# The DeltaNet's triangular inverses in 32x32 blocks, two per partition on DVE alone, joined to 128 by small TensorE products

## The chip, the cores and the metric

The kernel runs on one NeuronCore of a Trainium2 chip, as one launch. The metric is the time of that launch on the device in microseconds (us); three runs before gave a median of 2909.26 us (2909.12 to 2916.06). The engines are named as in the profile: PE is TensorE (matrix products), DVE is VectorE, ACT is ScalarE, POOL is GpSimd, SP is SyncE, whose queue issues most of the DMAs.

## The reference

A trunk of two layers for 256 tokens of width 2048, all in float32: the first layer mixes with MLA attention, the second with a gated DeltaNet; each is followed by a SwiGLU FFN and a gated embedding. The change lies in the DeltaNet, in the chunked delta rule, of which this is the core (32 value heads, 4 chunks of 64 tokens, head width 128):

```python
def chunk_gated_delta_rule(q, k, v, g, beta):
    ...                                        # C = 64 tokens a chunk
    decay = jnp.where(tril, jnp.exp(jnp.where(tril, diff, 0.0)), 0.0)
    L = jnp.where(strict, jnp.einsum('bhncd,bhnsd->bhncs', k_beta, k) * decay, 0.0)
    A = L + jnp.eye(C, dtype=f32)
    rhs = jnp.concatenate([v_beta, k_beta * jnp.exp(g)[..., None]], axis=-1)
    sol = lax.linalg.triangular_solve(A, rhs, left_side=True, lower=True, unit_diagonal=True)
    ...
    def step(state, inp):
        q_c, k_c, u_c, w_c, g_c, a_c = inp
        v_new = u_c - jnp.einsum('bhcd,bhde->bhce', w_c, state)
        o = (jnp.einsum('bhcd,bhde->bhce', q_c * jnp.exp(g_c)[..., None], state)
             + jnp.einsum('bhcs,bhse->bhce', a_c, v_new))
        ...
```

The kernel works with chunks of 128 tokens, two of them for the 256 tokens, which is the same mathematics. For each of 32 heads and 2 chunks it needs the inverse of I + L, where L is strictly lower triangular and 128x128: 64 such inverses.

## The kernel before

**The weights' products.** `linear` streams every weight matrix through the core. A tile `raw` of 4 x 128 rows by 512 columns (1 MB, three buffers) is loaded by SP. ACT rounds it to its high part `wh` (line 231), DVE subtracts to get the low part `wl` (line 232, "the split"), each in pieces of two k-tiles with five buffers. PE then makes twelve products a piece, three for each of two k-tiles and two token tiles (lines 240 to 242). After each piece `tick()` lets the generators in the lists `fill` and `back` put one more step of side work into the program. A scheduler then lays down one fixed order for each engine, and every engine runs its own in order. An evacuation takes the sums out of PSUM at the end of a block of 512 columns.

**The DeltaNet.** After the projections of q and k, `group` makes L^T for eight groups of four heads (tile `LT`) and stores the diagonal 64x64 blocks in DRAM as `Ld`, one block to a row of 128 (64 inverses, two blocks each), and the off-diagonal 64x64 blocks as `Md`. The next stretch of PE's work is the z projection in eight blocks (gg 0 to 7, the last one 256 columns wide, evacuated by `gate_z`) and the first block of the v projection, `first_v`. Beside it `lanes` computes the inverses of the 128 diagonal blocks by forward substitution, one 64x64 block to a partition: at each of 63 steps one product `pr` (line 790) and one difference `X` (line 792) over the rows below. The columns are divided: the first 12 (`KSPLIT`) go to DVE, the other 52 to POOL. ACT then copies the result out, transposed (`XT`) and straight (`XC`), and stores it as `XTd` and `Xd`.

**The joins and the scans.** For each group of eight inverses `tbuild` loads the two diagonal blocks of the inverse into `tt`, and with `d64` and `m64` makes the off-diagonal block by two stages of eight fp32 products in PE (line 824), with a copy by ACT (line 828) and one by DVE (line 831) behind them. A join for group gg + 2 is put into `back` when the scan of group gg nears its end. `scan` applies the delta rule to one group; the rest of the v projection and the output projection `w_out` run beside the scans.

Of the kernel before, what the change touches and what calls it, by code (L numbers as in the profile page):

```python
# [42 lines left out]
KSPLIT = 12  # L43
# [5 lines left out]
LAGX = 4  # L49
LSLOW = (8, 56)  # L50
# [16 lines left out]
def trunk(ctx: ExitStack, tc: tile.TileContext, a: dict, out, plan=("mla", "ffn", "ple", "gdn", "ffn", "ple"), first=0):  # L67
# [25 lines left out]
    # constants  # L93
# [10 lines left out]
    # residual stream  # L104
# [8 lines left out]
    # norm gains as columns  # L113
# [12 lines left out]
    def make_xT(src, gains):  # L126
        """src(t): [128 tokens, 512]; gives the two exact parts of its transpose times the gains, [128, 4, 256] each."""
# [36 lines left out]
    class Norm:  # L164
        """Parts of (h * gain)^T and, per token, 1/rms(h)."""
# [53 lines left out]
    def linear(xs, W, kt, blocks, evac, row0=0, need=None):  # L219
        """ps[t] = x[t] @ W[row0:, c0:c0+n] in float32, from exact 12-bit parts of both operands."""  # L220
# [38 lines left out]
    # ------------------------------------------------------------------ MLA  # L259
    def mla(j, nrm, nxt, mc):  # L260
# [6 lines left out]
        # rotary tables  # L267
# [26 lines left out]
        # upper bounds on scores: +BIG where a key may be seen, -BIG where not  # L294
# [6 lines left out]
        # latents  # L301
# [32 lines left out]
        # the keys' rotary part  # L334
# [138 lines left out]
    # ------------------------------------------------------------------ FFN  # L473
# [78 lines left out]
    # ------------------------------------------------------------------ GDN  # L552
    def gdn(j, nrm, nxt, mc, ctx):
# [20 lines left out]
        # tri[s, c] = 1 where s <= c  # L574
# [67 lines left out]
        def project(c0):  # L642
            """[tokens, 512] of the projection, before the convolution."""
# [32 lines left out]
        def l2(acc, dst):  # L676
            """dst = 1 / sqrt(sum of squares + eps) of the block's 4 heads; gives what is under the root."""
# [33 lines left out]
        def group(gg, rho, kap, E):  # L711
            """L^T and intra^T of value heads 4gg..4gg+3; rho, kap: [dk, 4 heads, 256 tokens]."""
# [59 lines left out]
        def lanes(pool):  # L772
            """Inverses of the 64x64 diagonal blocks of I + L, one per partition, by forward substitution."""
            L3 = pool.tile([P, 64, 64], F32, name="LL")
            nc.sync.dma_start(out=L3, in_=Ld)
            cols = []
            for eng, lo, hi in ((nc.vector, 0, KSPLIT), (nc.gpsimd, KSPLIT, 64)):
                X3 = pool.tile([P, 64, hi - lo], F32, name=f"X{lo}")
                nc.gpsimd.memset(X3, 0.0)
                nc.gpsimd.memset(X3.rearrange("p i k -> p (i k)")[:, lo * (hi - lo):hi * (hi - lo):hi - lo + 1], 1.0)  # L780
                cols.append((eng, lo, hi, X3, p4("pr")))
            for _ in range(8):
                yield
            for jj in range(63):
                ni = 63 - jj
                for eng, lo, hi, X3, pr in cols:
                    nk = min(jj + 1, hi) - lo
                    if nk > 0:
                        p3 = pr[:, 0:ni * nk].rearrange("p (i k) -> p i k", k=nk)
                        eng.tensor_mul(out=p3, in0=L3[:, jj, jj + 1:64].unsqueeze(2).to_broadcast([P, ni, nk]),  # L790
                                       in1=X3[:, jj, 0:nk].unsqueeze(1).to_broadcast([P, ni, nk]))
                        eng.tensor_sub(out=X3[:, jj + 1:64, 0:nk], in0=X3[:, jj + 1:64, 0:nk], in1=p3)  # L792
# [5 lines left out]
            for c in range(4):
                XT, XC = (p4(n).rearrange("p (a b) -> p a b", b=64) for n in ("XT", "XC"))
                b0 = 16 * c  # L800
                for _, lo, hi, X3, _ in cols:
                    s, e = max(lo, b0), min(hi, b0 + 16)
                    if s < e:
                        nc.scalar.copy(out=XT[:, s - b0:e - b0, :], in_=X3[:, :, s - lo:e - lo].rearrange("p i k -> p k i"))
                    nc.scalar.copy(out=XC[:, :, lo:hi], in_=X3[:, b0:b0 + 16, :])
                nc.scalar.dma_start(out=XTd[:, b0:b0 + 16, :], in_=XT)
                nc.scalar.dma_start(out=Xd[:, b0:b0 + 16, :], in_=XC[0:64])
                yield

        def tbuild(gg):  # L810
            """(I + L)^-T of a group's 8 chunks (head, chunk), from the inverses of the diagonal blocks."""
            tt = tts[gg % 2]
            for half in range(2):
                s, lane = slice(64 * half, 64 * half + 64), 64 * half + 8 * gg
                nc.sync.dma_start(out=tt[s, :, s], in_=XTd[lane:lane + 8].rearrange("m k i -> k m i"))
            nc.sync.dma_start(out=d64, in_=Xd[8 * gg:8 * gg + 8].rearrange("m i k -> i m k"))
            nc.sync.dma_start(out=m64[:, :, 64:128], in_=Md[gg])
# [13 lines left out]
            nc.vector.tensor_copy(out=tt[0:64, :, 64:128], in_=prods(64, w2[64:128], tt[64:128, :, 64:128], 64)[0:64])  # L831
# [48 lines left out]
        m64 = build.tile([64, 8, P], F32, name="m64")  # L880
# [182 lines left out]
```

## Time and profile before

| | before |
|---|---|
| median of three runs | 2909.26 us (2909.12 to 2916.06) |
| profiled execution: span from first to last instruction | 2911.4 us (the page gives no other time of it) |
| PE busy | 2829.5 us (97%), 13233 product records |
| DVE busy | 1733.8 us (60%) |
| ACT busy | 1368.2 us (47%) |
| POOL busy | 320.9 us (11%) |
| moved by DMA | 538.99 MB, 185 GB/s in the mean |

A product of `linear` is one record for PE; an fp32 product of the DeltaNet appears as two records. Records overlap, so a record's length is not its price; the price is the distance of two starts. Idle time of an engine that is not the bottleneck costs nothing.

### The profile page before, as it was taken

The page shows a single profiled execution, that of the slowest core. Times are in us where ns is not written, and L with a number is a line of the kernel's source. Part 1 is how long each engine was busy: PE and PEld are TensorE (multiplying, and loading weights), DVE is VectorE, ACT ScalarE, POOL GpSimd, SP SyncE. Part 2 cuts the span into 40 slices and gives each one's busy share as a digit, 9 for nine tenths or more (in the row PEclk, how much of TensorE's full clock was granted, in tenths as well). Part 3 has the DMA queues.
Part 4 walks back from the last instruction along what each step waited for, and adds up shares of the span by engine and source line. Part 5 has one row for each costly group of instructions (what it writes and reads, how often), then busy time and mean ns, then how long its engine had stood idle before and what let it go on. Part 6 is the DMA issues. An engine that isn't in the chain of part 4 may idle for free.

```text
span 2911.4 us, 33700 instructions
## 1 busy us (share of the span) xinstructions
PE 2829.5 (97%) x13233; PEld 2344.8 (81%) x13233; DVE 1733.8 (60%) x2112; ACT 1368.2 (47%) x1824; POOL 320.9 (11%) x358
## 2 busy tenths in 40 slices
PE   8999999999999999999957999999999999999999
PEld 8778888888888888778745788888888888888887
DVE  5665554544554666576799566767555554555654
ACT  6765444344344556555312544444544344434453
POOL 1330000000000000323696000000000000000000
PEclk9999999999999999999978999999999999999999
DMA  6335555555555555676623865554555555555554
GB/s 218 126 116 177 188 188 188 196 194 188 188 192 183 204 188 187 196 230 196 221 98 123 269 190 174 195 183 168 188 188 188 189 193 194 190 188 190 200 188 145
DMA packets 300241, 538.99 MB, mean 185 GB/s; under 512 B 39561, under 2 KB 60722, under 8 KB 299954
## 3 DMA queue, kind: packets, MB, share of 16 engines
q1 hardware_dynamic: 299186, 533.69, 55.6%
q10 hardware_dynamic: 896, 3.15, 0.3%
q8 instruction: 104, 1.70, 0.2%
q14 instruction: 55, 0.45, 0.0%
HBM read 516.84 MB, written 19.96 MB: 184 GB/s over the span
## 4 chain that ended last, share of the span: by engine, by line
PE 85%; DVE 7%; DMA 3%; ACT 2%; issue 1%; POOL 1%; SPq 0%; ACTq 0%; DVEq 0%; POOLq 0%
PE mm L240 26%; PE mm L242 26%; PE mm L241 26%; DVE wl L232 3%; DVE pr L790 2%; PE tr L135 2%; DVE X L792 1%; DMA raw<-in_gdn_w_in 1%; PE tr L917 1%; PE tr L824 1%; PE tr L923 1%; ACT wh L231 1%; PE tr L722 0%; PE S L412 0%; PE tr L660 0%
## 5 line engine op out<-in xcount | busy, mean ns | idle before, releaser
L232 DVE TENSOR_TENSOR wl<-raw,wh 128x1024 fp32r<-128x1024 f32 (+2 forms) x952 | 1176.3, 1240 | 982.1 <-ACT wh L231 976.4
L231 ACT CAST wh<-raw 128x1024 fp32r<-128x1024 f32 (+2 forms) x952 | 982.9, 1036 | 1306.4 <-PE mm L242 1178.2
L241 PE MATMUL mm<-wl,xh 128*128 128x512 f32 (+2 forms) x3776 | 1470.9, 390 | 51.8 <-DVE wl L232 51.5
L240 PE MATMUL mm<-wh,xh 128*128 128x512 f32 (+2 forms) x3776 | 1483.9, 393 | 5.2 <-ACT wh L231 5.1
L242 PE MATMUL mm<-wh,xl 128*128 128x512 f32 (+2 forms) x3776 | 1466.9, 389 | 0.0
L241 PEld LDWEIGHTS mm<-wl,xh 128*128 128x128 f32 x3776 | 715.6, 190 | 200.2 <-DVE wl L232 66.0
L240 PEld LDWEIGHTS mm<-wh,xh 128*128 128x128 f32 x3776 | 715.5, 190 | 149.0 <-ACT wh L231 6.2
L242 PEld LDWEIGHTS mm<-wh,xl 128*128 128x128 f32 x3776 | 715.4, 189 | 140.4 <-DVE xl L447 0.2
L102 POOL TENSOR_TENSOR re<-re,neghalf 128x2 f32<-128x2 f32 x2 | 1.4, 696 | 1350.2 <-DVE re L524 1350.2
L790 POOL TENSOR_TENSOR pr<-LL,X 128x51 f32<-128x51 f32 (+25 forms) x51 | 75.5, 1481 | 17.7 <-DMA LL<-Ld 13.8
L792 POOL TENSOR_TENSOR X<-X,pr 128x51 f32<-128x51 f32 (+25 forms) x51 | 73.4, 1439 | 4.0
L790 DVE TENSOR_TENSOR pr<-LL,X 128x240 f32<-128x240 f32 (+59 forms) x63 | 58.1, 923 | 4.0 <-DMA LL<-Ld 2.5
L792 DVE TENSOR_TENSOR X<-X,pr 128x240 f32<-128x240 f32 (+59 forms) x63 | 57.5, 913 | 1.5
L254 DVE TENSOR_TENSOR h<-h,mm 128x512 f32<-128x512 f32 x88 | 56.7, 680 | 2.3 <-PE mm L242 2.3
L144 ACT ACTIVATE xh<-tr,ncol 128x256 fp32r<-128x256 f32 x104 | 46.9, 475 | 19.6 <-PE tr L135 12.5
L145 DVE SCALAR_TENSOR_TENSOR xl<-tr,ncol,xh 128x256 fp32r<-128x256 f32 x104 | 47.4, 482 | 4.6 <-ACT xh L144 2.8
L102 POOL TENSOR_TENSOR rs<-rs,neghalf 128x2 f32<-128x2 f32 x6 | 4.8, 806 | 384.1 <-DVE rs L177 384.1
L970 POOL TENSOR_TENSOR r8o<-r8o,rq 128x8 f32<-128x8 f32 x8 | 5.2, 656 | 358.1 <-DVE r8o L966 358.1
L668 DVE SCALAR_TENSOR_TENSOR vT<-tr,cw,vT 128x255 f32<-128x255 f32 (+2 forms) x96 | 40.5, 473 | 0.4
L485 ACT ACTIVATE sg<-mm,rs 128x512 f32<-128x512 f32 x44 | 30.0, 690 | 20.8 <-PE mm L242 20.8
L157 ACT ACTIVATE junk<-h 128x512 f32<-128x512 f32 x48 | 29.9, 623 | 3.2 <-DMA h<-in_x 2.4
L489 DVE SCALAR_TENSOR_TENSOR md<-mm,rs,sg 128x512 f32<-128x512 f32 x44 | 30.9, 743 | 0.0
(257 smaller groups left out, 1377.0 us busy)
## 6 DMA issues: line engine op xcount, KB each, us to landing
raw<-in_ffn_w_gate_up SPq DMA_DIRECT2D x176, 1024.0 KB, 5.0
raw<-in_gdn_w_in SPq DMA_DIRECT2D x92, 1024.0 KB, 5.2
raw<-in_ffn_w_down SPq DMA_DIRECT2D x88, 1024.0 KB, 5.0
raw<-in_ple_w_gate SPq DMA_DIRECT2D x32, 1024.0 KB, 5.0
raw<-in_gdn_w_out SPq DMA_DIRECT2D x32, 1024.0 KB, 5.1
raw<-in_mla_w_o SPq DMA_DIRECT2D x16, 1024.0 KB, 5.1
raw<-in_mla_w_ukv SPq DMA_DIRECT2D x8, 1024.0 KB, 5.4
raw<-in_mla_w_in SPq DMA_DIRECT2D x8, 768.0 KB, 5.2
```

The source lines that it names most:

```text
L135: nc.tensor.transpose(out=ps[:, o:o + P], in_=src(t)[:, kk * P:(kk + 1) * P], identity=ident)
L144: nc.scalar.activation(out=xh[:, s], in_=ps[:, c:c + n], func=AF.Copy, scale=w)
L145: nc.vector.scalar_tensor_tensor(out=xl[:, s], in0=ps[:, c:c + n], scalar=w, in1=xh[:, s].bitcast(F32), op0=ALU.mult, op1=ALU.subtract)
L231: nc.scalar.copy(out=wh[:, :, :n], in_=raw[:, k2:k2 + 2, :n])
L232: nc.vector.tensor_sub(out=wl[:, :, :n], in0=raw[:, k2:k2 + 2, :n], in1=wh[:, :, :n].bitcast(F32))
L240: mm(ps[t][:, :n], lhsT=xh, rhs=wh[:, kk, :n], start=(k == 0), stop=False)
L241: mm(ps[t][:, :n], lhsT=xh, rhs=wl[:, kk, :n], start=False, stop=False)
L242: mm(ps[t][:, :n], lhsT=xl, rhs=wh[:, kk, :n], start=False, stop=(k == kt - 1))
L254: nc.vector.tensor_add(out=h[bi][:, t, :], in0=h[bi][:, t, :], in1=ps[t])
L668: nc.vector.scalar_tensor_tensor(out=acc[:, o + s:o + 256], in0=src[:, 0:256 - s], scalar=cw[:, jj * 64 + f:jj * 64 + f + 1], in1=acc[:, o ...
L790: eng.tensor_mul(out=p3, in0=L3[:, jj, jj + 1:64].unsqueeze(2).to_broadcast([P, ni, nk]), in1=X3[:, jj, 0:nk].unsqueeze(1).to_broadcast([P ...
L792: eng.tensor_sub(out=X3[:, jj + 1:64, 0:nk], in0=X3[:, jj + 1:64, 0:nk], in1=p3)
```

## The change

`lanes` now inverts 32x32 blocks. Each of the 128 partitions holds the two 32x32 diagonal blocks of one 64x64 block, and DVE alone does 31 steps over both at once. POOL has no part in it beyond two memsets. `group` stores the four diagonal 32x32 blocks of each L^T in `Ld` and all of L^T in `LTd` (for the 64x64 block in `Md`). `tbuild` loads L^T as `lt`, the four inverses into `tt` and three of them, straight, into `dd`, and joins in two levels: 32 to 64 by three sets of products of 32x32 blocks (five times eight products), and 64 to 128 by two sets of 64x64 blocks. The constants `KSPLIT`, `LAGX` and `LSLOW` go. Comments and docstrings are removed too, so line numbers shift by three or more (the products of `linear` are lines 237 to 239 in the changed kernel, the split 229, `pr` 782, `X` 784, the joins' products 814).

```diff
-        Md = [dram.tile([64, 8, 64], F32, name=f"Md{g}") for g in range(8)]
+        LTd = [dram.tile([P, 8, P], F32, name=f"LTd{g}") for g in range(8)]
...
-        Ld = dram.tile([P, 64, 64], F32, name="Ld")
-        Xd = dram.tile([64, 64, 64], F32, name="Xd")
-        XTd = dram.tile([P, 64, 64], F32, name="XTd")
+        Ld, Xd, XTd = (dram.tile([P, 2, 32, 32], F32, name=n) for n in ("Ld", "Xd", "XTd"))
...
             for half in range(2):
-                s, lane = slice(64 * half, 64 * half + 64), 64 * half + 8 * gg
-                nc.sync.dma_start(out=Ld[lane:lane + 8].rearrange("m j i -> j m i"), in_=l3[s, :, s])
-            nc.sync.dma_start(out=Md[gg], in_=l3[0:64, :, 64:128])
+                lane = 64 * half + 8 * gg
+                for q in range(2):
+                    s = slice(64 * half + 32 * q, 64 * half + 32 * q + 32)
+                    nc.sync.dma_start(out=Ld[lane:lane + 8, q].rearrange("m j i -> j m i"), in_=l3[s, :, s])
+            nc.sync.dma_start(out=LTd[gg], in_=l3)
...
         def lanes(pool):
-            for jj in range(63):
-                ni = 63 - jj
-                for eng, lo, hi, X3, pr in cols:
-                    nk = min(jj + 1, hi) - lo
...
+            L3 = pool.tile([P, 2, 32, 32], F32, name="LL")
+            nc.sync.dma_start(out=L3, in_=Ld)
+            X3 = pool.tile([P, 2, 32, 32], F32, name="X")
...
+            for jj in range(31):
+                ni, nk = 31 - jj, jj + 1
+                p3 = pr[:, 0:2 * ni * nk].rearrange("p (q i k) -> p q i k", q=2, k=nk)
+                nc.vector.tensor_mul(out=p3, in0=L3[:, :, jj, jj + 1:32].unsqueeze(3).to_broadcast([P, 2, ni, nk]),
+                                     in1=X3[:, :, jj, 0:nk].unsqueeze(2).to_broadcast([P, 2, ni, nk]))
+                nc.vector.tensor_sub(out=X3[:, :, jj + 1:32, 0:nk], in0=X3[:, :, jj + 1:32, 0:nk], in1=p3)
+                yield
+                yield
+            nc.scalar.dma_start(out=Xd, in_=X3)
+            for q in range(2):
+                XT = p4("XT").rearrange("p (a b) -> p a b", b=32)
+                nc.scalar.copy(out=XT, in_=X3[:, q].rearrange("p i k -> p k i"))
+                nc.scalar.dma_start(out=XTd[:, q], in_=XT)
...
         def tbuild(gg):
+            lt = p4("lt").rearrange("p (m c) -> p m c", c=P)
+            nc.sync.dma_start(out=lt, in_=LTd[gg])
             for half in range(2):
...
+                for q in range(2):
+                    s = slice(64 * half + 32 * q, 64 * half + 32 * q + 32)
+                    nc.sync.dma_start(out=tt[s, :, s], in_=XTd[lane:lane + 8, q].rearrange("m k i -> k m i"))
+                    if not half or not q:
+                        nc.sync.dma_start(out=dd[s, :, 32 * q:32 * q + 32],
+                                          in_=Xd[lane:lane + 8, q].rearrange("m i k -> i m k"))
...
+            for a in (0, 64):
+                A, B = slice(a, a + 32), slice(a + 32, a + 64)
+                minus(w1[B], prods(a + 32, lambda m: lt[A, m, B], lambda m: dd[A, m, 0:32], 32))
...
+            for a in (0, 64):
+                A, B = slice(a, a + 32), slice(a + 32, a + 64)
+                nc.vector.tensor_copy(out=tt[A, :, B], in_=prods(a, lambda m: w1[B, m, :], lambda m: tt[B, m, B], 32))
+            B = slice(32, 64)
+            nc.scalar.copy(out=dd[B, :, 0:32], in_=prods(32, lambda m: tt[B, m, B], lambda m: w1[B, m, :], 32))
...
-            w2 = build.tile([P, 8, 64], F32, name="w2")
-            nc.scalar.activation(out=w2[64:128], in_=prods(P, m64, d64, 64)[64:128], func=AF.Copy, scale=-1.0)
+            lo, up = slice(0, 64), slice(64, 128)
+            w2 = build.tile([P, 8, 64], F32, name="w2")
+            minus(w2[up], prods(64, lambda m: lt[lo, m, up], lambda m: dd[lo, m, :], 64))
...
+            nc.vector.tensor_copy(out=tt[lo, :, up], in_=prods(0, lambda m: w2[up, m, :], lambda m: tt[up, m, up], 64))
```

The order of DVE before, in the densest part of the lanes, around the steps on 588 to 564 elements (`wl` is the split, `pr` and `X` are the two operations of a step):

```order
L792 TENSOR_TENSOR X_10932<-X_10932,pr 128x600
L790 TENSOR_TENSOR pr<-LL,X_10932 128x588
L792 TENSOR_TENSOR X_10932<-X_10932,pr 128x588
L232 TENSOR_TENSOR wl<-raw,wh 128x1024
L790 TENSOR_TENSOR pr<-LL,X_10932 128x576
L792 TENSOR_TENSOR X_10932<-X_10932,pr 128x576
L232 TENSOR_TENSOR wl<-raw,wh 128x1024
L790 TENSOR_TENSOR pr<-LL,X_10932 128x564
L792 TENSOR_TENSOR X_10932<-X_10932,pr 128x564
L232 TENSOR_TENSOR wl<-raw,wh 128x1024
```

DVE after the change, around the largest steps:

```order
L784 TENSOR_TENSOR X<-X,pr 128x2x18x14
L782 TENSOR_TENSOR pr<-LL,X 128x510
L784 TENSOR_TENSOR X<-X,pr 128x2x17x15
L229 TENSOR_TENSOR wl<-raw,wh 128x1024
L782 TENSOR_TENSOR pr<-LL,X 128x512
L784 TENSOR_TENSOR X<-X,pr 128x2x16x16
L229 TENSOR_TENSOR wl<-raw,wh 128x1024
L782 TENSOR_TENSOR pr<-LL,X 128x510
L784 TENSOR_TENSOR X<-X,pr 128x2x15x17
L229 TENSOR_TENSOR wl<-raw,wh 128x1024
```

In both orders two or three lane operations stand before each split; the operations became a little smaller, POOL's have gone, and the steps are 31 for 63.

The order of PE before, in the first join (`m` and `d` are `m64` and `d64`, `w` is `w2`, `mm` rows are the weights' products, `vT` rows are transposes of the first scan):

```order
L824 MATMUL tr<-d_12329,m_12328 128x64 x8
L240 MATMUL mm<-wh,xh 128x512
L241 MATMUL mm<-wl,xh 128x512
L242 MATMUL mm<-wh,xl 128x512
L240 MATMUL mm<-wh,xh 128x512
L241 MATMUL mm<-wl,xh 128x512
L242 MATMUL mm<-wh,xl 128x512
L898 MATMUL tr<-ident,vT 128x128 x4
```

PE after the change, in the first join (`w` is `w1` here):

```order
L904 MATMUL tr<-ident,vT 128x128 x4
L814 MATMUL tr<-dd,lt 32x32 x16
L904 MATMUL tr<-ident,vT 128x128 x4
L814 MATMUL tr<-tt_12150,w_12271 32x32 x16
L814 MATMUL tr<-w_12271,tt_12150 32x32 x8
L238 MATMUL mm<-wl,xh 128x512
L239 MATMUL mm<-wh,xl 128x512
L237 MATMUL mm<-wh,xh 128x512
```

One set of eight products (and, twelve products later, a set of eight 64x64 ones) became sets of 16, 16 and 8 on 32x32 blocks; two sets of eight on 64x64 blocks follow further down. In the first join only four transposes stand between the first set and the second, which needs the first one's copy.

## Rows read from the trace of the kernel before

**Rows 1.** The page: busy shares, slices, costliest groups (busy, mean ns | idle before), DMA issues

```profile
PE 2829.5 (97%) x13233; PEld 2344.8 (81%) x13233; DVE 1733.8 (60%) x2112; ACT 1368.2 (47%) x1824; POOL 320.9 (11%) x358
...
PE   8999999999999999999957999999999999999999
...
L232 DVE TENSOR_TENSOR wl<-raw,wh 128x1024 fp32r<-128x1024 f32 (+2 forms) x952 | 1176.3, 1240 | 982.1 <-ACT wh L231 976.4
...
L241 PE MATMUL mm<-wl,xh 128*128 128x512 f32 (+2 forms) x3776 | 1470.9, 390 | 51.8 <-DVE wl L232 51.5
...
L790 DVE TENSOR_TENSOR pr<-LL,X 128x240 f32<-128x240 f32 (+59 forms) x63 | 58.1, 923 | 4.0 <-DMA LL<-Ld 2.5
L792 DVE TENSOR_TENSOR X<-X,pr 128x240 f32<-128x240 f32 (+59 forms) x63 | 57.5, 913 | 1.5
...
raw<-in_gdn_w_in SPq DMA_DIRECT2D x92, 1024.0 KB, 5.2
```

**Rows 2.** Windows: stretch, length, busy PE, PEld, DVE, ACT, POOL, clock, DMA, GB/s

```profile
1415.34:1636.90 221.56, 169.12 (x675) 129.43 (x673) 195.39 (x179) 71.89 (x80) 149.47 (x103) 0.89 0.47 154
...
1426.00:1606.00 180.00, 129.43 (x481) 96.71 (x480) 177.37 (x158) 46.69 (x52) 142.20 (x90) 0.87 0.36 113
```

**Rows 3.** Groups of DVE by shape, 1430 to 1570 us (count | busy, mean ns)

```profile
L232 DVE TENSOR_TENSOR wl<-raw,wh 128x1024 fp32r<-128x1024 f32 x25 | 55.9, 2234 | 0.0
...
L790 DVE TENSOR_TENSOR pr<-LL,X 128x540 f32<-128x540 f32 x2 | 3.4, 1686 | 0.0
```

**Rows 4.** Timeline of DVE after POOL's part has ended (start, length, instruction)

```profile
1576.18 0.47 DVE L790 TENSOR_TENSOR pr<-LL,X 128x312 f32<-128x312 f32 x1
...
1602.59 0.17 DVE L790 TENSOR_TENSOR pr<-LL,X 128x12 f32<-128x12 f32 x1
```

**Rows 5.** Timeline at both ends of the stretch ([idle before <- releaser])

```profile
1415.34 1.37 ACT L586 ACTIVATE sz<-mm,rs 128x512 f32<-128x512 f32 x2 [0.99 <-PE mm L242]
...
1637.56 1.45 PE L660 MATMUL tr<-ident,xs 128*128 128x128 f32 x8 [0.64 <-ACT xs L247]
```

**Rows 6.** Timeline of PE: starts of undisturbed weight products, 512 and 256 columns

```profile
1394.73 0.39 PE L240 MATMUL mm<-wh,xh 128*128 128x512 f32 x1
...
1411.74 0.39 PE L240 MATMUL mm<-wh,xh 128*128 128x512 f32 x1
...
1610.43 0.28 PE L240 MATMUL mm<-wh,xh 128*128 128x256 f32 x1
...
1611.87 0.28 PE L240 MATMUL mm<-wh,xh 128*128 128x256 f32 x1
```

**Rows 7.** All waits of PE from 1640 to 2080 us (total, times, longest)

```profile
PE tr L824 <- DMA tt<-XTd: 1.0, 1, 1.0
PE mm L241 <- DVE wl L232: 0.5, 1, 0.5
```

**Rows 8.** Timeline around two blocks of a join, a scan's products and a copy

```profile
1657.73 0.40 PE L242 MATMUL mm<-wh,xl 128*128 128x512 f32 x1
1658.06 1.14 PE L824 MATMUL tr<-tt,w 64*64 64x64 f32 x16
...
1659.69 0.40 PE L242 MATMUL mm<-wh,xl 128*128 128x512 f32 x1
...
1661.71 0.59 ACT L930 COPY vn<-tr 128x512 f32<-128x512 f32 x1 [4.63 <-PE tr L917]
...
1671.04 1.02 PE L923 MATMUL tr<-S,KQl 128*128 128x256 f32 x4
...
1730.40 0.39 PE L242 MATMUL mm<-wh,xl 128*128 128x512 f32 x1
...
1732.64 0.50 PE L240 MATMUL mm<-wh,xh 128*128 128x512 f32 x1
```

**Rows 9.** Waits of SP's queue from 1640 to 2080 us (total, times, longest)

```profile
SPq L227 <- DVE wl L232: 259.0, 47, 10.8
...
SPq L816 <- PE tr L824: 24.8, 7, 9.0
```

More of the change, by code (lines that the diff above doesn't have):

```diff
@@ L42 @@
 RB = 3
-KSPLIT = 12
 NV0 = 1
@@ L48 @@
 KY = 3
-LAGX = 4
-LSLOW = (8, 56)
 P2 = {"mla": 14, "gdn": 8, "ffn": 6, "ple": 6}
@@ L772, in lanes @@
         def lanes(pool):
-            L3 = pool.tile([P, 64, 64], F32, name="LL")
+            L3 = pool.tile([P, 2, 32, 32], F32, name="LL")
             nc.sync.dma_start(out=L3, in_=Ld)
[L776 to L781, printed above, removed]
+            X3 = pool.tile([P, 2, 32, 32], F32, name="X")
@@ L782, in lanes @@
+            nc.gpsimd.memset(X3, 0.0)
+            nc.gpsimd.memset(X3.rearrange("p q i k -> p q (i k)")[:, :, 0:1024:33], 1.0)
+            pr = p4("pr")
             for _ in range(8):
                 yield
-            for jj in range(63):
-                ni = 63 - jj
-                for eng, lo, hi, X3, pr in cols:
-                    nk = min(jj + 1, hi) - lo
[L788 to L792, printed above, removed]
+            for jj in range(31):
[4 more added lines that the diff above has]
+                nc.vector.tensor_sub(out=X3[:, :, jj + 1:32, 0:nk], in0=X3[:, :, jj + 1:32, 0:nk], in1=p3)
@@ L793, in lanes @@
                 yield
-                if LSLOW[0] <= jj < LSLOW[1]:
-                    yield
-            for _ in range(LAGX):
                 yield
[L798 to L807, printed above, removed]
+            nc.scalar.dma_start(out=Xd, in_=X3)
@@ L812, in tbuild @@
             tt = tts[gg % 2]
+            lt = p4("lt").rearrange("p (m c) -> p m c", c=P)
+            nc.sync.dma_start(out=lt, in_=LTd[gg])
             for half in range(2):
[L814 to L817, printed above, removed]
+                lane = 64 * half + 8 * gg
+                for q in range(2):
[4 more added lines that the diff above has]
+                                          in_=Xd[lane:lane + 8, q].rearrange("m i k -> i m k"))
@@ L818, in tbuild, with prods @@
             for _ in range(6):
                 yield
-            def prods(rows, lhs, rhs, n):
+            def prods(o, lhs, rhs, n):
                 ps = trp()
                 for m in range(8):
-                    mm(ps[0:rows, m * n:(m + 1) * n], lhsT=lhs[:, m, :], rhs=rhs[:, m, :], start=True, stop=True)
-                return ps.rearrange("p (m c) -> p m c", c=n)
-            w2 = build.tile([P, 8, 64], F32, name="w2")
-            nc.scalar.activation(out=w2[64:128], in_=prods(P, m64, d64, 64)[64:128], func=AF.Copy, scale=-1.0)
+                    mm(ps[o:o + n, m * n:(m + 1) * n], lhsT=lhs(m), rhs=rhs(m), start=True, stop=True)
+                return ps[o:o + n, 0:8 * n].rearrange("p (m c) -> p m c", c=n)
@@ L829, in tbuild, with minus @@
+            def minus(dst, src):
+                nc.scalar.activation(out=dst, in_=src, func=AF.Copy, scale=-1.0)
+            w1 = build.tile([P, 8, 32], F32, name="w1")
+            for a in (0, 64):
+                A, B = slice(a, a + 32), slice(a + 32, a + 64)
+                minus(w1[B], prods(a + 32, lambda m: lt[A, m, B], lambda m: dd[A, m, 0:32], 32))
             yield
             yield
-            nc.vector.tensor_copy(out=tt[0:64, :, 64:128], in_=prods(64, w2[64:128], tt[64:128, :, 64:128], 64)[0:64])
+            for a in (0, 64):
+                A, B = slice(a, a + 32), slice(a + 32, a + 64)
+                nc.vector.tensor_copy(out=tt[A, :, B], in_=prods(a, lambda m: w1[B, m, :], lambda m: tt[B, m, B], 32))
@@ new lines, in tbuild @@
+            B = slice(32, 64)
[5 more added lines that the diff above has]
+            minus(w2[up], prods(64, lambda m: lt[lo, m, up], lambda m: dd[lo, m, :], 64))
+            yield
+            yield
+            nc.vector.tensor_copy(out=tt[lo, :, up], in_=prods(0, lambda m: w2[up, m, :], lambda m: tt[up, m, up], 64))
@@ L879, in gdn @@
         tts = [build.tile([P, 8, P], F32, name=f"tt{i}") for i in range(2)]
-        m64 = build.tile([64, 8, P], F32, name="m64")
-        d64 = build.tile([64, 8, 64], F32, name="d64")
-        for z in (*tts, m64):
+        dd = build.tile([P, 8, 64], F32, name="dd")
+        for z in (*tts, dd):
             nc.gpsimd.memset(z, 0.0)
```

## The prediction, made before the changed kernel had run

> **What bounds the kernel now.** I read the busy shares and the 40 slices first. TensorE (PE) is busy for 97% of the span, and its digits are 9 nearly everywhere; they fall to 5 and 7 in slices 21 and 22 alone [rows 1]. So time is to be had almost only in that stretch; everywhere else a microsecond of PE work that is added is a microsecond of span. The windows come next: from 1426 to 1606 us PE is busy for 129.4 of 180 us, at a granted clock of 0.87 in the mean (between its two levels, 1.2 and 2.4 GHz), while DVE is busy for 177.4 and POOL for 142.2, and the DMA share falls to 0.36 [rows 2]. The costliest groups say who is late: the products of line 241 wait 51.5 us in the whole run for `wl`, the low part of the weights that DVE makes [rows 1]. And `wl` is late because DVE is full: one split takes 2.23 us there, against 1.24 in the mean of the run, and a lane operation of 540 elements takes 1.69 us [rows 1, 3]. The same kind of operation after POOL has ended shows what DVE needs alone: 0.47 us for 312 elements, 0.17 for 12 [rows 4]. So the bound here is the inverses on DVE and POOL together, each slowing the other, with the splits queued in order between them.
>
> **What the stretch loses.** It runs from the end of projection gg1's products (ScalarE's evacuation starts at 1415.34) to the end of `first_v`, where PE stops at 1637.56 - 0.64 = 1636.9 [rows 5]: 221.6 us. In it PE has six projections of 96 products of 512 columns, and one of 96 products of 256. Undisturbed, 75 products lie between 1394.73 and 1411.74, 0.2268 us each, and 12 narrow ones between 1610.43 and 1611.87, 0.120 each [rows 6]. That makes 6 x 96 x 0.2268 + 96 x 0.120 = 130.6 + 11.5 = 142.1 us, so 79.5 us are lost. Nearly all of the 51.5 us of waits lie here; most of the rest is the lower clock.
>
> **Part 1, the lanes.** Removed: 126 DVE operations (58.1 + 57.5 = 115.6 us) and POOL's 102, nearly all of its 149.5 us in the stretch [rows 1, 2]. Added: 31 steps of two DVE operations on 2(31-j)(j+1) elements each, 10,912 elements for the products and as many for the differences. By [rows 4] an operation costs (0.47 - 0.17)/300 = 1.0 ns an element over about 0.16 us, so 21,824 x 1.0 ns + 62 x 0.16 us = 31.7 us, the largest (512 elements) 0.67 us. POOL is out, so I take this undisturbed price; the pattern of two blocks has no row of its own, and its upper bound is the disturbed price, 1.69 us at 540 elements, its lower one the flat price itself. Do the splits queued behind these operations come in time? In the changed order 19 splits stand between the first and the last lane operation: 19 x 1.2 + 31.7 = 54.5 us of DVE, against 19 x 12 x 0.2268 = 51.7 us that PE takes for their products, plus the five splits made ahead (13.6 us of PE work). In the densest part, as the rows of the order show, two or three lane operations of 0.67 us and a split make 2.5 to 3.2 us against 2.72. The lead sinks by the 4.3 us of the first six steps and then stays near 4 us. I take no wait of PE: -79.5 us. At the disturbed price 31.7 becomes about 80 us, and some 35 us of the loss would stay.
>
> After the lanes the inverses go out in three DMAs in place of eight, and two strided copies on ScalarE take the place of thirteen. At present PE waits behind that: 0.64 us for `xs` [rows 5], 1.0 for `tt` and 0.5 for `wl` [rows 7]. The lanes should now end near 1472 (1418 + 54), some 85 us before `first_v` does. I take -2.0 us.
>
> **Part 2, the joins.** This is PE work in a stage where PE waits 1.5 us in 440 [rows 7], so all of it is paid, eight times. I price a block by how far it pushes the weights' products apart, its switches in and out included [rows 8]. Before: around the 128x64 block 1732.64 - 1730.40 = 2.24 us, less one step of 0.23, and 0.1 for a longer step behind it: 2.1 us. Around the 64x64 block 1659.69 - 1657.73 = 1.96 us, less three steps (0.68): 1.28 us. A join costs 3.4 us. After: blocks of 16, 24 (16 and 8 together), 8 and 8 products; an fp32 product is two records. The last two blocks are 64x64: 2 x 1.28. For 32x32 there is no row. The records of 64x64 start (1.14 - 0.22)/15 = 61 ns apart, those of 256 columns (1.02 - 0.38)/3 = 213 ns [rows 8] (0.22 and 0.38 are what the last record lasts): nearly in proportion to the columns, with a few ns over. Above, a record of 32 columns costs what one of 64 does, 61 ns; below, half and the few ns, 33. What a block costs beyond its records is 1.28 - 16 x 0.061 = 0.31 us. With 32 and 48 records the first two blocks cost 2.26 + 3.24 us above and 1.37 + 1.89 below, the join 8.1 or 5.8 us, the change +4.7 or +2.4 us, eight joins +37 or +19. The ends are not far apart, and the rows speak for neither floor nor proportion below 64 columns, so I take the middle, 47 ns: +28 us.
>
> The Trainium skill has a rule that speaks against the change here: in TensorEngine Tiling (Array Packing), Performance Considerations (Instruction Overhead), a matmul of one column is said to take as long as one of 60, so that nothing is won on a side that is small already. By that rule the upper end holds, +37 us; no row here shows it. The skill's TensorE: Matmul & The Clock Gate (Wait — 56ns, not 53.3ns?) puts the least distance of two starts at about 25 ns, which leaves the lower end open.
>
> New waits on PE: each stage of a join needs the copy of the stage before, and behind the waiting product stand the weights' products and the whole scan. The order puts 4 to 24 other products between the stages, mostly 1 us or more, against a copy of 0.59 us (a 512-wide one [rows 8]); only in the first join do a mere four transposes, some 0.5 us, stand between the first and the second. +1.5 us for the eight, bounds 0 and 5.
>
> **Part 3, transfers.** A join issues 8 DMAs for 4, all on SP: 32 more, in a queue that mostly waits for buffers [rows 9]. L goes out whole, 512 KB a group for 128, and is read back: 6 MB more; `LL` shrinks from 2 MB to 1. The DMA share in the stretch is 0.36 to 0.47 [rows 2], so I cost this at nothing; the cover is the lead of the raw tiles, and rival 4 is what it costs without.
>
> **The sum.** Against the profiled span of 2911.4 us: -79.5 - 2.0 + 28 + 1.5 = -52, so 2859.4 us. That span is 2.1 us over the median of the runs (2909.26), and the page gives no other time of that execution; taken off, 2857 us. About 0.3% (9 us) is what a measurement of this kernel can tell from no change.
>
> **Rivals.** 1. *A product of 32 columns costs as much as one of 64* (the rule above): +37 for +28, 2866 us. For it: none of the rows has like records closer than 61 ns. Against it: from 256 to 64 columns the price follows the columns. 2. *The lanes still bind on DVE*: the splits stand behind two-block operations that cost half again what flat ones do, 47 us for 31.7; the lead of 4 us is gone and PE waits some 12 us: 2869 us. For it: the demand is 54.5 against 51.7 us. Against it: nothing in [rows 4] is slow without POOL. 3. *DVE was not the cause*: the weights' loads keep the stretch slow, and half the loss stays: 2897 us. For it: the DMA share is lowest there. Against it: SP's longest waits are for `wl` [rows 9], so the loads are late because DVE is. 4. *The loads of the joins hold up the weights* (the other side): SP works in order, `dd` is a single buffer, and its next load must wait until the fourth stage of the join before has read it; the weights' loads stand behind. Such a wait reaches 9.0 us now [rows 9]. Three raw tiles of 5.44 us of products each, less 5.2 us for a load [rows 1], give 11 us of lead, so it decides from there; waits of 20 us at seven joins would cost 7 x 9 = 63 us: 2920 us. Against it: the order puts these loads late, between the weights' loads.
>
> **Chances.** Forecast (records between 33 and 55 ns, lanes hidden) 0.56; rival 1 0.23; rival 2 0.10; rival 3 0.05; rival 4 0.03; better than the lowest sum 0.03. The lowest sum has +19 and no new waits, 2847 us; a few us under it for gains that no row shows give 2840. The upper end takes in rivals 1 and 2 together, 2878. So the range of 8 in 10 is 2840 to 2878. Faster 0.94, same 0.02, slower 0.04; rival 3 is still 12 us faster than before.
>
> **What would show it.** POOL's busy time in the stretch falls to next to nothing, and DVE's lane operations to some 32 us; the splits there take 1.2 us; no PE digit falls below 9 after the lanes start; the waits for `wl` all but vanish; from gg1's end to `first_v`'s end it is 142 us. PE has 640 more records, and a join's blocks take 5.8 to 8.1 us together. The prediction is wrong if splits still take 1.5 us or more beside the lanes, or if PE waits for raw tiles or copies in the scans.

## The result, and the profile after

The changed kernel takes 2845.63 us (median of four runs, 2844.79 to 2846.78) beside 2910.22 us for the kernel before (2909.12 to 2916.06): a ratio of 0.9772, 95% interval 0.9758 to 0.9786. Run once more with the experiments, it took 2845.22 us. The profiled execution has a span of 2843.8 us, 67.6 less than before.

The page of the kernel after, the lines that answer to [rows 1] (busy us, share and instructions; slices in tenths; groups with busy, mean ns, idle time before them):

```profile
PE 2819.0 (99%) x13873; PEld 2347.5 (83%) x13873; DVE 1633.4 (57%) x2064; ACT 1370.4 (48%) x1837; POOL 168.7 (6%) x254
PE   8999999999999999999999999999999999999999
L229 DVE TENSOR_TENSOR wl<-raw,wh 128x1024 fp32r<-128x1024 f32 (+2 forms) x952 | 1149.7, 1211 | 1014.1 <-ACT wh L228 1013.4
L238 PE MATMUL mm<-wl,xh 128*128 128x512 f32 (+2 forms) x3776 | 1460.2, 387 | 0.0
```

The hole in PE's slices is gone, the products with `wl` wait for nothing (51.5 us before), and PE has the 640 records more. Windows of the kernel after, which answer to [rows 2]: the stretch from gg1's end to `first_v`'s end, and 180 us from the same start:

```profile
core 0: us, PE busy (x) PEld busy (x) DVE busy (x) ACT busy (x) POOL busy (x), PEclk, DMA share, GB/s
1413.27:1555.37 142.10, 142.10 (x673) 119.63 (x672) 93.24 (x119) 67.15 (x73) 2.32 (x3) 1.00 0.75 249
1413.27:1593.27 180.00, 180.00 (x944) 151.02 (x943) 114.65 (x151) 86.39 (x98) 2.32 (x3) 1.00 0.72 241
```

PE is busy throughout and the granted clock is 1.00, where it was 129.4 of 180 us at 0.87. The ends of the stretch, as in [rows 5], from ScalarE's timeline of the kernel after (start, duration, line, operation, what ended the idle time):

```profile
1413.27 1.37 ACT L583 ACTIVATE sz<-mm,rs 128x512 f32<-128x512 f32 x2 [0.98 <-PE mm L239]
...
1555.37 1.37 ACT L244 ACTIVATE xs<-mm,rs 128x512 f32<-128x512 f32 x2 [0.99 <-PE mm L239]
```

That is 142.1 us for 221.6. DVE's groups of the kernel after between 1413 and 1470 us, and the largest lane operations on its timeline:

```profile
L229 DVE TENSOR_TENSOR wl<-raw,wh 128x1024 fp32r<-128x1024 f32 x22 | 26.8, 1220 | 2.3 <-ACT wh L228 2.3
L784 DVE TENSOR_TENSOR X<-X,pr 128x62 f32<-128x62 f32 (+15 forms) x31 | 16.3, 526 | 0.8
L782 DVE TENSOR_TENSOR pr<-LL,X 128x62 f32<-128x62 f32 (+15 forms) x31 | 16.2, 523 | 0.7
...
1439.37 0.68 DVE L782 TENSOR_TENSOR pr<-LL,X 128x512 f32<-128x512 f32 x1
1440.09 0.69 DVE L784 TENSOR_TENSOR X<-X,pr 128x512 f32<-128x512 f32 x1
```

The lanes cost 32.5 us of DVE (31 products and 31 differences). A split takes 1.22 us between them, against 2.23 in [rows 3].

The joins, which answer to [rows 8], on PE's timeline of the kernel after (a row is a run of like records; its duration ends with the last record's):

```profile
1621.52 0.39 PE L239 MATMUL mm<-wh,xl 128*128 128x512 f32 x1
1621.84 1.09 PE L814 MATMUL tr<-dd,lt 32*32 32x32 f32 x32
1622.86 0.50 PE L237 MATMUL mm<-wh,xh 128*128 128x512 f32 x1
1623.20 0.40 PE L238 MATMUL mm<-wl,xh 128*128 128x512 f32 x1
...
1629.64 0.19 PE L814 MATMUL tr<-w,tt 32*32 32x32 f32 x1
1629.64 0.19 PE L814 MATMUL tr<-tt,w 32*32 32x32 f32 x1
...
1662.77 0.69 PE L814 MATMUL tr<-w,tt 32*32 32x32 f32 x16
```

The first block pushes the products apart by 1622.86 - 1621.52 = 1.34 us, less a step of 0.23, and 0.1 for the longer step behind it: 1.2 us. Measured in the same way each 64x64 block costs 1.29 us, and the second stage (`tt,w` and `w,tt`) 1.6 in the first three joins, where its three sets stand in one block. In the other five the third set stands in a block of its own (the last row), and the two blocks cost some 2.0 us. So a join costs 5.4 to 5.8 us where it cost 3.4.

The span can be cut at the starts of the weights' products, which are the same 11,424 in each kernel. Two pieces, in us, worked out from the traces, stand beside the median time: the 600 products that begin near 1411 us (beside the lanes), and the 1,100 that begin shortly behind `first_v` (beside the scans, with all the joins):

| kernel | 600 products beside the lanes | 1,100 products with the joins | median time |
|---|---|---|---|
| before | 202.27 | 344.67 | 2910.22 |
| after | 125.78 | 360.53 | 2845.63 |
| e3, POOL busy | 195.33 | 360.58 | 2914.38 |
| e10, POOL copies | 181.75 | 362.08 | 2901.46 |
| e9, POOL writes only | 125.78 | 360.69 | 2846.76 |
| e4, before with DVE alone | 125.78 | 376.41 | 2862.19 |
| e5, lanes' products three times | 132.08 | 360.60 | 2853.14 |
| e2, 32x32 products twice | 125.78 | 386.01 | 2870.94 |
| e6, 64 columns | 125.78 | 374.29 | 2856.76 |
| e8, L twice | 125.78 | 360.56 | 2844.59 |
| e1, interleaved | 125.78 | 356.47 | 2840.60 |
| e7, one PSUM tile | 125.78 | 351.29 | 2838.09 |
| e11, copy on DVE | 125.78 | 349.88 | 2836.09 |

### The profile page after: what moved, and what is told of

Read it like the earlier page. It is cut to its first block, busy times and chain, and to the rows that moved or that the text cites. A ratio compares the mean times of both kernels' runs of the same rounds, so it can differ in the third digit from the quotient of the medians.

```text
span 2843.8 us, 34910 instructions
## 1 busy us (share of the span) xinstructions
PE 2819.0 (99%) x13873; PEld 2347.5 (83%) x13873; DVE 1633.4 (57%) x2064; ACT 1370.4 (48%) x1837; POOL 168.7 (6%) x254
## 4 chain that ended last, share of the span: by engine, by line
PE 92%; DVE 3%; ACT 2%; DMA 1%; POOL 1%; issue 1%; SPq 0%; DVEq 0%; ACTq 0%; POOLq 0%
PE mm L237 28%; PE mm L239 28%; PE mm L238 28%; PE tr L132 2%; PE tr L814 1%; DVE wl L229 1%; PE tr L923 1%; PE tr L929 1%; DMA raw<-in_gdn_w_in 1%; ACT wh L228 1%; PE S L409 0%; PE tr L657 0%; PE S L408 0%; PE tr L681 0%; POOL E L734 0%
## 5 line engine op out<-in xcount | busy, mean ns | idle before, releaser
L229 DVE TENSOR_TENSOR wl<-raw,wh 128x1024 fp32r<-128x1024 f32 (+2 forms) x952 | 1149.7, 1211 | 1014.1 <-ACT wh L228 1013.4
L137 ACT CAST xh<-tr 128x512 fp32r<-128x512 f32 x44 | 23.8, 588 | 14.9 <-PE tr L132 14.9
L138 DVE TENSOR_TENSOR xl<-tr,xh 128x512 fp32r<-128x512 f32 x44 | 28.5, 685 | 2.1
L982 DVE SCALAR_TENSOR_TENSOR vb<-vb,r8o,zg 128x128 f32<-128x128 f32 x64 | 17.5, 346 | 19.9 <-POOL r8o L979 19.9
L244 ACT ACTIVATE xs<-mm,rs 128x512 f32<-128x512 f32 x32 | 21.5, 686 | 14.1 <-PE mm L239 14.0
```

The source lines that it names most:

```text
L229: nc.vector.tensor_sub(out=wl[:, :, :n], in0=raw[:, k2:k2 + 2, :n], in1=wh[:, :, :n].bitcast(F32))
```

## The experiments

**Was it POOL, or the amount of work on DVE?** e3 gives POOL back its 102 operations on a scratch tile:

```diff
+            Y3 = pool.tile([P, 64, 52], F32, name="Y")
...
+            py = p4("py")
...
+                    y3 = py[:, 0:ni * nk].rearrange("p (i k) -> p i k", k=nk)
+                    nc.gpsimd.tensor_mul(out=y3, in0=Y3[:, jj + 1:64, 0].unsqueeze(2).to_broadcast([P, ni, nk]),
+                                         in1=Y3[:, jj, 0:nk].unsqueeze(1).to_broadcast([P, ni, nk]))
+                    nc.gpsimd.tensor_sub(out=Y3[:, jj + 1:64, 0:nk], in0=Y3[:, jj + 1:64, 0:nk], in1=y3)
```

> The kernel after, with 102 operations on POOL beside the lanes, of the shapes that POOL had before, on a scratch tile that nothing reads. DVE, PE, the joins and the transfers are unchanged. Theory (POOL and DVE slow each other): beside POOL a split takes 1.8 us or more for 1.22, the lane operations twice their 0.67 us, DVE needs 19 x 2.0 + 65 = 103 us where PE takes 51.7, and PE waits 25 to 45 us for wl: 2870 to 2890. Rival (it was the amount of work that left DVE): splits stay at 1.22 us and PE waits for nothing, 2846.

Measured: 2914.38 us (2911.51 to 2917.11), ratio to before 1.0012 (1.0002 to 1.0021). The whole gain is gone. The trace of e3: its window, the splits in it, PE's longest wait, and two neighbours on DVE with POOL's operation beside them:

```profile
1413.00:1570.00 157.00, 111.73 (x387) 84.57 (x386) 144.62 (x92) 42.29 (x44) 133.68 (x91) 0.85 0.43 143
...
L229 DVE TENSOR_TENSOR wl<-raw,wh 128x1024 fp32r<-128x1024 f32 x33 | 61.3, 1876 | 11.0 <-ACT wh L228 10.9
...
PE mm L238 <- DVE wl L229: 45.3, 17, 5.0
...
1438.08 2.27 DVE L229 TENSOR_TENSOR wl<-raw,wh 128x1024 fp32r<-128x1024 f32 x1
1440.28 1.76 DVE L794 TENSOR_TENSOR pr<-LL,X 128x440 f32<-128x440 f32 x1
...
1439.35 2.22 POOL L789 TENSOR_TENSOR Y<-Y,py 128x595 f32<-128x595 f32 x1
```

DVE has no more to do than after, and yet a split takes 2.27 us while POOL works. The stretch loses 69.5 us, more than the 25 to 45 expected: 45.3 us are waits for `wl`. The other 24 us are a lower clock: PE is busy for 111.7 us with 387 records, which at 0.2268 us each would take 87.8, and the granted clock is 0.85 in the mean of this window (1.00 after). It was POOL.

e4 is the other side: the kernel before, its 64x64 inverses on DVE alone.

```diff
-KSPLIT = 12
+KSPLIT = 64
...
-            for eng, lo, hi in ((nc.vector, 0, KSPLIT), (nc.gpsimd, KSPLIT, 64)):
+            for eng, lo, hi in ((nc.vector, 0, KSPLIT),):
```

> The kernel before, its 64x64 inverses on DVE alone in place of 12 columns on DVE and 52 on POOL; POOL is out, the joins are as before. DVE has 126 operations on 174,720 elements together... worked out: 2 x 43,680 products and as many differences make 87,360 elements at 1.0 ns and 126 x 0.16 us, some 108 us undisturbed, for the 115.6 us of its disturbed share before. Theory (contention): splits take 1.22 us; DVE needs 108 us and 52 splits x 1.22 = 63 us, 171 us against 142.1 us of products less a lead of 8.5 us, so 20 to 30 us are lost in place of 79.5: 2855 to 2865 us. Rival (amount of DVE's work): 108 for 115.6 us changes little, 2900 to 2910.

Measured: 2862.19 us (2861.28 to 2862.71), ratio 0.9832 (0.9817 to 0.9846). Its groups on DVE from 1413 to 1595 us, the one large wait on PE that it has more, the last product before that wait, and ScalarE's first copy behind the lanes and what stands behind its last:

```profile
L792 DVE TENSOR_TENSOR X<-X,pr 128x63 f32<-128x63 f32 (+31 forms) x63 | 55.4, 879 | 1.0
L790 DVE TENSOR_TENSOR pr<-LL,X 128x63 f32<-128x63 f32 (+31 forms) x63 | 55.3, 878 | 3.3 <-DMA LL<-Ld 2.3
...
PE tr L660 <- ACT xs L247: 29.7, 1, 29.7
...
1578.59 0.39 PE L242 MATMUL mm<-wh,xl 128*128 128x512 f32 x1
...
1594.38 1.91 ACT L804 COPY XT<-X 128x1024 f32<-128x1024 f32 x1 [14.32 <-DVE X L792]
...
1607.97 1.27 ACT L247 ACTIVATE xs<-mm,rs 128x512 f32<-128x512 f32 x2 [0.53 <-ACT XC L805]
```

Nearly as much DVE time as before (110.7 us for 115.6), and the 600 products lose nothing. So about three quarters of the gain, 48 of 64.6 us, was to be had from taking POOL out, with no other block size. The time lies in the expected 2855 to 2865 us by luck: that range was worked out from late splits, and there are none. What is lost is lost by a lateness of a different kind: the lanes end at 1594.4 us, 15 us after PE has run out of products, and 13.6 us of copies stand on ScalarE between them and `first_v`'s evacuation. PE waits 29.7 us once. The smaller blocks buy just that, for a dearer join: less the wait, e4's 1,100 products take 346.7 us, 14 less than after.

**What on POOL gets in the way?** Two more kernels have 102 operations of 1024 elements on POOL that write constants (e9, the second line below) or copy (e10, the third, in its place).

```diff
+                    for _ in range(2):
+                        nc.gpsimd.memset(py, 0.0)
+                        nc.gpsimd.tensor_copy(out=py, in_=y)
```

> As e3_pool_busy, but POOL's 102 operations write 1024 constants each and read nothing (0.95 us each by a like row of the trace after, some 97 us in all, over the whole of the lanes). Theory (POOL and DVE share what they read through): splits stay at 1.22 us, PE waits for nothing, 2846 us. Rival (any work of POOL slows DVE, or its instructions alone do): by e3's loss of 69.5 us for 142 us of POOL, 97 us of POOL cost some 47: 2893 us.

> As e3_pool_busy, but POOL's 102 operations copy 1024 elements each from a tile to another (one input). Theory (what both read through is shared, so one input is enough): splits take 1.8 us or more while POOL copies, and by e3's rate (half a microsecond lost for one of POOL) 100 to 150 us of POOL cost 48 to 72: 2893 to 2917. Rival (only operations with two inputs on POOL get in DVE's way): splits at 1.22, 2846.

Measured: e9 2846.76 us (2842.81 to 2847.93), ratio 0.9774 (0.9759 to 0.9790); e10 2901.46 us (2899.45 to 2904.95), ratio 0.9968 (0.9955 to 0.9980). POOL's group from 1410 us on and the splits from 1415 to 1570 us, first of e9:

```profile
L786 POOL MEMSET py<- 128x1024 f32 x97 | 92.8, 956 | 5.4
...
L229 DVE TENSOR_TENSOR wl<-raw,wh 128x1024 fp32r<-128x1024 f32 x53 | 64.5, 1222 | 39.7 <-ACT wh L228 39.7
```

and then of e10, with PE's wait:

```profile
L787 POOL COPY py<-Y 128x1024 f32<-128x1024 f32 x99 | 146.4, 1479 | 6.1
...
L229 DVE TENSOR_TENSOR wl<-raw,wh 128x1024 fp32r<-128x1024 f32 x37 | 69.2, 1883 | 8.2 <-ACT wh L228 8.0
...
PE mm L238 <- DVE wl L229: 35.9, 19, 4.5
```

POOL is busy for 93 us in e9 and no split is longer for it; in e10 one input is enough. What slows DVE is that POOL reads. The Trainium skill has this rule in SBUF — State Buffer (Who interferes with whom): an instruction of VectorE with two inputs in SBUF contends with one of GpSimd that reads SBUF, not with one that only writes. These three runs agree on POOL's side: a split takes 1.22 us in the mean in e9, and 1.88 in e10 and in e3, a few undisturbed ones counted in. On DVE's side the splits and the lanes all have two inputs; that an operation with one would be spared is shown by no run here.

**How much DVE work is hidden?** e5 makes each product of the lanes three times (these two lines are added twice).

```diff
+                nc.vector.tensor_mul(out=p3, in0=L3[:, :, jj, jj + 1:32].unsqueeze(3).to_broadcast([P, 2, ni, nk]),
+                                     in1=X3[:, :, jj, 0:nk].unsqueeze(2).to_broadcast([P, 2, ni, nk]))
```

> Each product of the lanes is made three times on DVE (62 more operations, 31.7 us more of DVE by the prediction's price), with no more ticks between them; nothing of it reaches the result. Theory (DVE alone is fast, and the lead of 7.2 us that the trace after shows is all that covers it): DVE needs 19 x 1.22 + 64 = 87 us where PE takes 51.7, so PE waits about 27 us: 2873. Rival (only POOL beside DVE makes the splits late; this amount of DVE work is hidden): under 5 us, 2846 to 2850.

Measured: 2853.14 us (2850.76 to 2854.72), ratio 0.9804 (0.9788 to 0.9820). Neither number. PE's wait that is new, and ScalarE's row of that time:

```profile
PE mm L237 <- ACT sz L583: 4.4, 1, 4.4
...
1524.21 3.79 ACT L794 COPY XT<-X 128x1024 f32<-128x1024 f32 x2 [4.23 <-DVE X L788]
1526.20 2.15 ACTq L795 DMA_DIRECT2D XTd<-XT  x2
1528.40 2.42 ACT L583 ACTIVATE sz<-mm,rs 128x512 f32<-128x512 f32 x4 [0.40 <-ACT XT L794]
```

No product waits for `wl`: with longer lanes the scheduler lays down another order, with 38 splits among the lane operations in place of 19, and the shortest lead of a split over its products is 4.8 us (5.4 after). The expectation took the order of the kernel after for fixed, and that was its mistake. What costs 6.3 us is that the two copies of `XT` now stand together ahead of an evacuation: 4.4 us are the wait, and the rest is a lower clock right behind it (0.84 in the mean from 1524 to 1535 us). So with the lanes at twice their DVE time (65 us), in the order that the scheduler then gives, DVE still does not bind.

**What does a small product cost?** e2 issues each 32x32 product twice (the first two lines below), e6 widens 64 of the 80 records of a join to 64 columns (the last line).

```diff
-                for m in range(8):
+                for m in [m for m in range(8) for _ in range(2 if n == 32 else 1)]:
...
+                    mm(ps[o:o + 32, m * 64:(m + 1) * 64], lhsT=lhs(m), rhs=rhs(m), start=True, stop=True)
```

> Every 32x32 product is issued twice (640 more records, no more blocks or copies). Theory, 32 ns a record as the trace after shows: +20.5 us, 2866. By the prediction's middle of 47 ns: +30, 2876. By the floor of rival 1, 61 ns: +39, 2885.

> In a join the two first-stage sets and the two tt,w sets (64 records) take 64 columns in place of 32, with the same 32 rows and 32 output rows; the added columns are not used. If the price of a record is its columns, their starts move from 32 to 58 or 60 ns apart: 64 x 27 ns = 1.7 us a join, +14 us, 2859. If it is a price per instruction (rival 1 in another form) or the 32 rows: nothing, 2846.

Measured: e2 2870.94 us (2864.69 to 2872.70), ratio 0.9858 (0.9844 to 0.9873); e6 2856.76 us (2856.02 to 2857.25), ratio 0.9818 (0.9803 to 0.9832). The first block of the third join, first in e2:

```profile
1627.13 2.11 PE L814 MATMUL tr<-dd,lt 32*32 32x32 f32 x64
```

and then in e6:

```profile
1623.24 1.78 PE L820 MATMUL tr<-dd,lt 32*32 32x64 f32 x32
```

After, 32 records take 1.09 us; 32 more add 1.02, that is 32 ns each. By 640 records that is the 20.5 us expected. The 1,100 products lost 25.5. Nearly all of the other 5 is a lower clock: behind some of the doubled blocks the weights' products start 0.43 us apart for 0.23, as at the lower level (1.2 GHz), though PE was busy throughout. Of the four runs the one with the highest clock (0.996, for 0.994 and 0.995) took 2864.69 us, near the 2866 expected. The windows of the 1,100 products, of after and of e2, and two such products of e2:

```profile
1559.96:1920.49 360.53, 360.32 (x2478) 298.77 (x2476) 227.67 (x356) 168.30 (x222) 19.28 (x28) 1.00 0.53 174
...
1558.68:1944.69 386.01, 385.99 (x3117) 323.58 (x3116) 229.03 (x356) 168.62 (x222) 19.27 (x28) 0.98 0.49 162
...
1872.48 0.63 PE L238 MATMUL mm<-wl,xh 128*128 128x512 f32 x1
1872.91 0.63 PE L239 MATMUL mm<-wh,xl 128*128 128x512 f32 x1
```

In e6 the same 32 records with double the columns add 0.69 us, and the 1,100 products lose 13.8 us for the 14 expected. The price follows the columns; the floor of rival 1, 61 ns, isn't there.

**Are the transfers hidden?** e8 stores and reads each L^T twice.

```diff
+            nc.sync.dma_start(out=LTe[gg], in_=l3)
...
+            nc.sync.dma_start(out=lt2, in_=LTe[gg])
```

> Each group's L is stored twice and read back twice (16 more DMAs of 512 KB, 8 MB more; the second copy is read by nothing). Prediction's term (transfers are hidden): no change, 2845.6 us within 1. Rival 4 in weak form (they hold up SP's queue or the weights' loads): more than 5 us.

Measured: 2844.59 us (2843.50 to 2848.25), ratio 0.9778 (0.9764 to 0.9793): nothing.

**A faster join.** In the trace after, records start 32 ns apart within a set, but in pairs some 5 ns apart where two sets meet that lie in different rows and columns of the array (1629.64 in the joins' rows above). e1 makes the sets alternate:

```diff
-            for a in (0, 64):
-                A, B = slice(a, a + 32), slice(a + 32, a + 64)
-                minus(w1[B], prods(a + 32, lambda m: lt[A, m, B], lambda m: dd[A, m, 0:32], 32))
...
+            pss = [trp() for _ in sets]
+            for m in range(8):
+                for ps, (o, lhs, rhs) in zip(pss, sets):
+                    mm(ps[o:o + 32, m * 32:(m + 1) * 32], lhsT=lhs(m), rhs=rhs(m), start=True, stop=True)
```

> The 32x32 products of a join are issued in turn over the positions of the array (blocks 0 and 64 alternating in the first stage, the three sets alternating in the second); same products, same records. Theory: in the trace after, like records of 32 columns start 32 ns apart, but 5 ns apart where the next lies in another position, so alternating records overlap: the first block of 32 records falls from 1.24 us to about 0.75, the second of 48 from 1.62 to about 0.8, a join is 1.3 us shorter, the time 2835 us. Rival: 32 ns is the price of a record wherever it lies, and the 5 ns only an accident of how two sets meet: no change, 2845.6 us.

Measured: 2840.60 us (2840.15 to 2842.72), ratio 0.9759 (0.9745 to 0.9774): half of what was expected. PE's timeline of e1, a first stage, and the third set of a later join:

```profile
1618.49 0.69 PE L821 MATMUL tr<-dd,lt 32*32 32x32 f32 x32
...
1658.14 0.69 PE L821 MATMUL tr<-w,tt 32*32 32x32 f32 x16 [0.63 <-DVE xl L142]
```

The 32 records take 0.69 us for 1.09, so they do overlap. The Trainium skill says in TensorEngine Tiling (Array Packing) (Key Properties) that different tiles of the array can run matmuls in parallel, and this row agrees. But in five joins the third set stands alone and waits, 3.2 us in all: with a PSUM tile for each set, the stage needs three of the four at once. e7 is e1 with the sets of a stage in one.

```diff
-            pss = [trp() for _ in sets]
+            ps = trp()
```

> As e1_interleave, with the two or three sets of a stage in one PSUM tile (their output rows are different) in place of one tile each. In e1 the third set stood apart and waited for a free PSUM tile: from the third join on, the second stage cost 2.3 to 2.5 us in two pieces where the first stage cost 0.84. Theory (the missing half of e1's gain is this wait): the second stage becomes one block of some 0.9 us, 1.2 us less at five or six joins, 2834 us. Rival (records that write one bank from two positions of the array do not overlap, or the rest of e1's gain is lost elsewhere): the stages go back to 1.24 and 1.6 us and the time to 2845, or stay at e1's 2840.6.

Measured: 2838.09 us (2835.26 to 2838.33), ratio 0.9752 (0.9737 to 0.9766). Its 1,100 products take 9.2 us less than after, 5.2 less than e1. The medians differ by 2.5 alone, as the first of the 600 products starts 2.9 us later in e7 than in e1; the median is 4 over the 2834 expected. The first and the last record of a second stage in e7, all 48 between them:

```profile
1659.05 0.22 PE L821 MATMUL tr<-tt,w 32*32 32x32 f32 x2
...
1659.56 0.19 PE L821 MATMUL tr<-w,tt 32*32 32x32 f32 x1
```

The one wait for the joins that PE has there is 2.3 us in two joins, for ScalarE's copy into `dd`. e11 is e7 with that copy on DVE, ahead of the two copies into `tt`.

```diff
-            nc.scalar.copy(out=dd[B0, :, 0:32], in_=q2)
+            nc.vector.tensor_copy(out=dd[B0, :, 0:32], in_=q2)
```

> As e7_one_bank, with the copy into dd on DVE, ahead of the two copies into tt, in place of ScalarE, for which PE waited 1.2 us at two joins there. Theory: these 2.3 us go and nothing else, 2835.8. Rival (DVE has splits queued ahead of the copy, so the wait only changes its engine): 2838 or more.

> The changed kernel once more, on the same chip and beside the same runs of before as e11, so that the two can be compared directly: 2845.6 us, and by the theory of overlapping records 7 to 10 us more than e11.

Measured on one chip: e11 2836.09 us (2834.55 to 2836.40), ratio 0.9742 (0.9729 to 0.9756); the changed kernel 2845.22 us (2843.22 to 2847.00), ratio 0.9773 (0.9759 to 0.9787). PE's wait for `dd` in e11:

```profile
PE tr L814 <- DVE dd L838: 0.8, 2, 0.4
```

e11 is the fastest kernel here, 9.1 us under the changed one, and their runs don't overlap; the two ratios' intervals do not either. Of the copy itself (e7 to e11) the traces show that the wait falls from 2.3 to 0.8 us and the 1,100 products take 1.4 less; the 2.0 us of the medians come from different sets of runs and are not told from nothing.

## Why the prediction was right, and where its size was off

2857.0 us was predicted, 2845.6 measured, inside the range of 2840 to 2878; the forecast of faster held. In spans the sum gave -52 us and the traces give -67.6, 15.6 us apart: 11.1 of them are the joins, 1.5 the new waits, 2.1 an earlier start of the stretch, and 0.9 lie behind `first_v` unexplained. That the times are only 11.4 apart is luck: the sum took 2.1 us off the span to come to a median, but here a run takes 1.7 us more than its span (2845.54 and 2843.8).

- **The lanes, -79.5 us: right.** 221.6 to 142.1 us. The flat price held for the pattern of two blocks (32.5 us for 31.7; 0.68 us for 0.67), and POOL was the cause (e3, e4). The upper bound was low: at the disturbed price some 35 us of the loss were to stay, and e3 loses 69.5, as the splits are longer too and the clock falls. The lead was 5.4 us at the least, not near 4 (the terms that the prediction names, 13.6 less 4.3, would leave 9.3; it does not say what takes the rest). The lanes ended at 1467.5, not 1472, as they started at once; they took 54.0 us for 54.5.
- **The joins, +28 us: mis-sized, and this is most of the difference.** From `first_v`'s end to the end of the span it is 2911.4 - 1636.9 = 1274.5 us before and 2843.8 - 1555.37 = 1288.4 after: +13.9, where 28 - 2.0 + 1.5 = +27.5 stood. The 1,100 products give +15.9; before, they hold 1.0 us of waiting for `tt`, so the eight joins cost +16.9, 2.1 each for the 3.5 taken. The step that failed is the middle of 33 and 61 ns. A record of 32 columns costs 32 ns (e2) and the row of 64 had already been nearly in proportion to that of 256, so the lower end was the likelier. The joins came out below even that end (+17 for +19), because two sets overlap where they meet: the first block costs 1.2 us for 1.37. In five joins the second stage is two blocks, not the one of the prediction, which takes a part of that away.
- **Rival 1, a floor near 60 columns: not there.** Records of 32 columns start 32 ns apart, those of 64 columns 58 to 61, and 256 columns take 213 ns [rows 8], two cycles a column at 2.4 GHz (the granted clock is 1.00 there). The Trainium skill states the rule in TensorEngine Tiling (Array Packing), Instruction Overhead, in columns (one as long as 60) and as some 60 cycles of overhead. In columns it does not hold for these records, and the measurement decides. Its 60 cycles would be 25 ns at 2.4 GHz, an estimate from that figure of the Trainium skill. A record of 32 columns already takes 32 ns here, so no run shows whether records in one position of the array have a floor of that size; records in different positions have none (48 within 0.51 us in e7, 11 ns apart in the mean).
- **New waits, +1.5 us: none.** PE's waits after have no row for the joins. The copies come in time even in the first join.
- **XT and the tail, -2.0 us: right.** PE's waits for `xs` (0.64), `tt` (1.0) and `wl` (0.5), 2.1 us in all, have no row after. 13.9 less 16.9 is -3.0; the 0.9 that is left is not explained.
- **Transfers, 0: right** (e8). Rival 4 falls because PE's waits after have no row at all from 1556 to 2080 us, rival 2 by the lanes' 32.5 us (it had 47) and the missing waits for `wl`, rival 3 by the 142.1 us.
- Not in the sum: the stretch starts 2.1 us earlier after than before. In the kernels made from the changed one the first of the 600 products starts between 1407.6 and 1413.2 us, so this is left unexplained.

## What to carry to other kernels

Before a job is divided between DVE and POOL, ask whether DVE's operations there have two inputs in SBUF and POOL's read it: then work given to POOL is not off DVE's back, as here, and what is queued on DVE pays for it. Look next at what waits for DVE, and at when the side job must be done; e4 shows that taking POOL out was worth three quarters of the gain by itself, and the smaller blocks only had to bring the end forward. Where small products can lie in different rows and columns of the array, issue them in turn, with one PSUM tile for the lot.

## What the runs showed that was not expected

- POOL's 102 operations on scratch data cost 69.5 us of a 142 us stretch, though nothing waits for them (e3); 93 us of writing constants in the same place cost nothing (e9).
- fp32 records of 32x32 start 32 ns apart; 32 of them in two positions of the array take 0.69 us in turn and 1.09 one set behind the other, and 48 in three positions, in one PSUM tile, start within 0.51 us (e7).
- Twice as much DVE time in the lanes made PE wait for no split (e5): the scheduler's order moved with it.
- With twice as many 32x32 records in the joins the granted clock was 0.98 over the 1,100 products for 1.00, though PE was busy throughout, and nearly 5 us went with it (e2).
